# Tiles 8 to 31 of the up projection split into high and low parts by two GpSimd DMAs and a ScalarE negation

## The chip, the cores and the metric

The kernel runs on one core of a Trainium2 chip. The metric is the device time of one execution in microseconds (us). Three timed runs of the kernel before gave 833.49, 833.70 and 833.92 us; the median is 833.7 us.

## The reference

One layer of an encoder on a 512 x 1024 input, all in float32: a token-mixing sub-layer with three branches (windowed attention, spatial gating, causal pooling), a cross-attention into 256 memory tokens, and a squared-ReLU MLP, each between RMSNorms. The change touches the MLP alone:

```
hf = rmsnorm(x, g_norm[l, 4])                                # 512 x 1024
yf = jnp.square(jax.nn.relu(hf @ w_up[l])) @ w_down[l]       # w_up 1024 x 4096, w_down 4096 x 1024
x = x + rmsnorm(yf, g_norm[l, 5])
```

## The kernel before

Every matrix product is made of three TensorE products in the type float32r. An operand w is split into hi (w rounded to float32r) and lo (w minus hi), and `mm3` (L137 to 141) adds hi·hi, hi·lo and lo·hi in PSUM. The split of a weight tile is `split` (L129 to 131): a rounding copy on ScalarE writes hi, a subtraction on VectorE writes lo.

A weight tile has 128 partitions by 1024 float32 values, 512 KB. `wtile` (L112 to 119) loads it from HBM with a DMA on SyncE's queue into one of 2 buffers `wraw` and splits it into one of 8 buffers `whi` and one of 8 buffers `wlo`. The same 8 + 8 buffers also hold the operands of the second product of the MLP: the activations `ahi`, `alo` and the weights `bhi`, `blo`.

The first product of the MLP has 32 weight tiles (here U0 to U31), each 128 of the 4096 hidden features. U0 to U5 run on halves of the 512 rows and are written out by hand. From U6 on, a list `steps` orders the work: a step U makes one tile of hidden features (24 matmuls of 512 columns, then a Relu and a Square on ScalarE, L735 and L736). A step M is one of seven products of a Strassen-like scheme for the second product, for one of three groups of 8 hidden tiles (24 matmuls of 512 columns as well; its operands are sums made on VectorE and three tiles that are split, two of which are weights). In the middle of a group U and M alternate; at two places two U or two M follow each other, and U28 to U31 follow each other near the end. Then come C (sums on VectorE) and D0 and D1, the last quarter of the second product, done plainly, with eight further weight tiles through `wtile`. Four steps X at the beginning of the list transpose the residual x.

The loop over `steps` traces `prepare` for step n + 2 ahead of the matmuls of step n, so a step's tiles have their place in the buffers two steps ahead. TensorE's instructions are pinned to the order in which they are traced (`keep`, L97). The order on the other engines is made by a scheduler at compile time: it takes the work in order of priority as its inputs become ready by its own estimate of durations. Each engine, and each engine's DMA queue, runs its list in that order and waits in place.

Up to the last steps, GpSimd has small work only (a power for the norms, some sums of squares), and every DMA is issued on SyncE's queue.

Of the kernel before, what the change touches and what calls it, by code (L numbers as in the profile page):

```python
# [10 lines left out]
F32 = mybir.dt.float32  # L11
F32R = mybir.dt.float32r
AF = mybir.ActivationFunctionType
ALU = mybir.AluOpType
AX = mybir.AxisListType

P = 128
# [31 lines left out]
T_UP = T_OM + 4  # L49
# [12 lines left out]
def trunk(ctx: ExitStack, tc: tile.TileContext, xT, memT, wst, cst, vec, rows, wsp, wpl, out):  # L62
    nc = tc.nc

    per = ctx.enter_context(tc.tile_pool(name="per", bufs=1))
    wp = ctx.enter_context(tc.tile_pool(name="wp", bufs=1))
# [11 lines left out]
    def slot(name, dt=F32, shape=None):  # L78
        return sl.tile(shape or [P, S], dt, name=name, tag="slot", bufs=NSLOT)
# [7 lines left out]
    def pair(name, shape=None):  # L87
        return slot(name + "h", F32R, shape), slot(name + "l", F32R, shape)
# [16 lines left out]

    wdma = {}

    def wtiles(i):
        return [wp.tile([P, 1024], dt, name=f"w{c}{i}", tag=f"w{c}", bufs=n)
                for c, dt, n in (("raw", F32, 2), ("hi", F32R, 8), ("lo", F32R, 8))]  # L110

    def wtile(i, fence=()):  # L112
        raw, hi, lo = wtiles(i)
        wdma[i] = nc.sync.dma_start(raw, wst[i]).ins
        with ExitStack() as c:
            for ins in fence:
                c.enter_context(tc.issue_after(ins))
            split(hi, lo, raw)
        return hi, lo

    def after(i, dst, src):
# [7 lines left out]
    def split(hi, lo, src, order=free):  # L129
        return (order(nc.scalar.copy(hi, src)).ins,  # L130
                order(nc.vector.tensor_tensor(lo, src, hi.bitcast(F32), op=ALU.subtract)).ins)  # L131
# [62 lines left out]
    with ExitStack() as c1:  # L194
# [17 lines left out]
        for o in order:  # L212
            if o[0] == "x":
                nc.sync.dma_start(x0[o[1]], xT[o[1] * P:(o[1] + 1) * P, :])
            else:
                c = slice(o[2] * 512, (o[2] + 1) * 512)
# [4 lines left out]
        for o in order:  # L221
            if o[0] == "x":
                split_scaled(*xg[o[1]], x0[o[1]], vc[:, V_G + o[1]:V_G + o[1] + 1], keep)
            else:
                c = slice(o[2] * 512, (o[2] + 1) * 512)
# [8 lines left out]
        def block(i, w=None, fence=()):  # L234
            ps = bank()
            gemm(w or wtile(i, fence), xg, 0, KD, ps)
            return ps
# [103 lines left out]
        def vgate(t):  # L341
            if not wsv:
                wsv.extend(wtile(T_SV + i, fence(8 + NU0 + i)) for i in range(4))
            ps = bank()
            for k in range(KD):
                mm3(ps, cut(xg[k], t * P, (t + 1) * P), blk(wsv[k // 2], k % 2, 512), k == 0, k == KD - 1)
            vn.append(ps)
# [65 lines left out]
        def branch(n, y, sg):  # L413
            for d in range(KD):
                if d % 2 == 0:
                    w = wtile(T_BR + n * 4 + d // 2)
                ps = bank()
                gemm(w, y, 4 * (d % 2), 4, ps)
                if n == 0:
                    acc[d] = slot(f"acc{d}")  # L420
                    nc.vector.tensor_tensor(acc[d], sg[d], ps, op=ALU.mult)
                else:
                    nc.vector.tensor_tensor(sg[d], sg[d], ps, op=ALU.mult)
                    nc.vector.tensor_tensor(acc[d], acc[d], sg[d], op=ALU.add)
                if n == 2:
                    mg.append(pair(f"mg{d}"))
                    split(*mg[d], acc[d])
# [297 lines left out]
    with ExitStack() as c3:  # L725
        f = c3.enter_context(tc.tile_pool(name="f", bufs=1))
# [46 lines left out]
        def whole(name):  # L773
            return f.tile([P, 1024], F32, name=name, tag="q", bufs=8)
# [26 lines left out]
        def loads(g, *quarters):  # L801
            for ab in quarters:
                for pp in range(2):
                    i = T_DN + 8 * g + 4 * ab[0] + 2 * ab[1] + pp
                    qs[g, ab, pp] = whole(f"q{ab[0]}{ab[1]}")
                    wdma[i] = nc.sync.dma_start(qs[g, ab, pp], wst[i]).ins

        def halves(g, a):
            return rel[g, a][:, :, :HALF], rel[g, a][:, :, HALF:]
# [6 lines left out]
        def ready(g, i):  # L816

            def q(ab, pp):
                return qs[g, ab, pp]

            def new(name):
                sums[g, name] = f.tile([P, NPAIR, HALF], F32, name=name, tag="s", bufs=2)
                return sums[g, name]

            a0, a1 = halves(g, 0)
            if i == 1:
                first, second = a0, (0, 0)
            if i == 7:
                first, second = new("s3"), (0, 1)
                sub(first, a0, a1)  # L830
                for pp in range(2):
                    sub(q((0, 0), pp), q((0, 1), pp), q((0, 0), pp))
                    sub(q((0, 1), pp), q((1, 1), pp), q((0, 1), pp))
            if i > 1 and i != 7:
                b0, b1 = halves(g, 1)
            if i == 5:
                first, second = new("s1"), (0, 0)
                add(first, a1, b1)
            if i == 6:
                first, second = new("s2"), (0, 0)  # L840
                sub(first, sums[g, "s1"], a0)
                for pp in range(2):
                    sub(q((0, 0), pp), q((1, 1), pp), q((0, 0), pp))
            if i == 4:
                first, second = b1, (0, 0)
                for pp in range(2):
                    sub(q((0, 0), pp), q((0, 0), pp), q((1, 0), pp))
            if i == 3:
                first, second = sums[g, "s2"], (1, 1)
                sub(first, b0, first)  # L850
            if i == 2:
                first, second = b0, (1, 0)
            act, ws = parts(first, i), []
            for pp in range(2):
                w = tuple(wp.tile([P, 1024], F32R, name=f"b{z}{i}", tag=f"w{z}", bufs=8) for z in ("hi", "lo"))
                split(*w, q(second, pp))
                ws.append(w)
            return act, ws
# [71 lines left out]

        def prepare(st):
            if st[0] == "U":
                return wtile(T_UP + st[1])
            if st[0] == "D":
                a = st[1]
                if a == 0:
                    gy.extend(slot(f"gy{c}") for c in range(2))
                    for c in range(2):
                        nc.sync.dma_start(gy[c], rows[0:1, 1032 + c * 512:1032 + (c + 1) * 512].broadcast_to([P, 512]))
                if a == 0:  # L940
                    act = [tuple(f.tile([P, NPAIR, HALF], F32R, name=f"e{c}", tag="q", bufs=8) for c in "hl")
                           for _ in range(2)]
                    for z, src in zip(act, halves(3, a)):
                        split(*z, src)
                else:
                    act = [pair(f"e{j}") for j in range(4)]
                    for j in range(4):
                        split(*act[j], rel[3, a][:, j, :])
                ws = [wtile(T_DN + 24 + 4 * a + j) for j in range(4)]
                if a == 0:  # L950
                    for t in range(NT):
                        xt[t] = whole(f"xt{t}")
                        nc.sync.dma_start(xt[t], xd[t * P:(t + 1) * P, :])
                return act, ws
            if st[0] == "M":
                g, i = st[1:]
                if st[1:] == (0, 1):
                    loads(0, (0, 0), (0, 1), (1, 1), (1, 0))
                got = ready(g, i)
                if i == 4 and g < 2:  # L960
                    loads(g + 1, (0, 0), (0, 1))
                if i == 2 and g < 2:
                    loads(g + 1, (1, 1), (1, 0))
                return got

        got = {}
        for n in range(-2, len(steps)):
            if n >= 0 and steps[n] == ("D", 0):
                got[n + 1] = prepare(steps[n + 1])
            if n + 2 < len(steps) and n + 2 != len(steps) - 1:  # L970
                got[n + 2] = prepare(steps[n + 2])
            if n < 0:
                continue
            st = steps[n]
            if st[0] == "X":
                xturned(st[1])
            elif st[0] == "U":
                up(st[1], got.pop(n))
            elif st[0] == "M":
                product(st[1], st[2], *got.pop(n))  # L980
            elif st[0] == "C":
                combine()
            else:
                down(st[1], *got.pop(n))
# [79 lines left out]
```

## Time and profile before

| | |
|---|---|
| median of 3 runs | 833.7 us (833.49 to 833.92) |
| the profiled execution | 833.36 us |
| its span, first to last instruction | 831.6 us |
| mean granted TensorE clock over the span | 0.998 of full speed |
| busy share of the span: TensorE, VectorE, ScalarE, GpSimd | 98%, 66%, 48%, 5% |
| DMA | 88.65 MB, 107 GB/s on average |

Times in the rows are microseconds from the span's start, unless marked ns. PE is TensorE's matmul, PEld its weight load, DVE VectorE, ACT ScalarE, POOL GpSimd, SPq SyncE's queue of DMA issues. "L130" is line 130 of the kernel before. In a row of a timeline the brackets hold the time for which the engine sat idle ahead of the instruction, and what ended that wait.

### The profile page before, as it was taken

The page shows a single profiled execution, that of the slowest core. Times are in us where ns is not written, and L with a number is a line of the kernel's source. Part 1 is how long each engine was busy: PE and PEld are TensorE (multiplying, and loading weights), DVE is VectorE, ACT ScalarE, POOL GpSimd, SP SyncE. Part 2 cuts the span into 40 slices and gives each one's busy share as a digit, 9 for nine tenths or more (in the row PEclk, how much of TensorE's full clock was granted, in tenths as well). Part 3 has the DMA queues.
Part 4 walks back from the last instruction along what each step waited for, and adds up shares of the span by engine and source line. Part 5 has one row for each costly group of instructions (what it writes and reads, how often), then busy time and mean ns, then how long its engine had stood idle before and what let it go on. Part 6 is the DMA issues. An engine that isn't in the chain of part 4 may idle for free.

```text
span 831.6 us, 11071 instructions
## 1 busy us (share of the span) xinstructions
PE 817.6 (98%) x4322; PEld 700.3 (84%) x4322; DVE 544.9 (66%) x795; ACT 399.5 (48%) x696; POOL 45.2 (5%) x55
## 2 busy tenths in 40 slices
PE   8999999999999999999999999999999999999996
PEld 6888888888788888899999999788888888888885
DVE  6559893667536535718897793694719682997436
ACT  7344568432422333536466765676626452644502
POOL 0000000000000010103300041000000000000000
PEclk9999999999999999999999999999999999999999
DMA  7332112533222333402342220653421430116302
GB/s 245 127 102 76 51 54 98 186 119 102 76 102 81 121 127 102 178 1 77 102 149 102 81 78 26 254 184 136 159 77 52 158 120 26 51 44 234 103 0 102
DMA packets 27845, 88.65 MB, mean 107 GB/s; under 512 B 3344, under 2 KB 4368, under 8 KB 27792
## 3 DMA queue, kind: packets, MB, share of 16 engines
q1 hardware_dynamic: 27792, 87.94, 31.0%
q8 instruction: 34, 0.56, 0.3%
q14 instruction: 19, 0.16, 0.1%
HBM read 83.73 MB, written 4.19 MB: 106 GB/s over the span
## 4 chain that ended last, share of the span: by engine, by line
PE 88%; DVE 6%; ACT 2%; DMA 1%; issue 1%; POOL 0%; SPq 0%; POOLq 0%; DVEq 0%; ACTq 0%
PE ps L100 87%; PE ps L103 2%; DVE x L552 1%; DVE yg L551 1%; DVE wlo L131 1%; DVE m L917 1%; DVE m L799 1%; DMA q<-wst 1%; DMA x<-xT 1%; ACT sq L903 1%; ACT sq L162 0%; DVE sa L163 0%; DVE xm6l L135 0%; POOL rst L914 0%; POOL rs L176 0%
## 5 line engine op out<-in xcount | busy, mean ns | idle before, releaser
L130 ACT CAST whi<-wraw 128x1024 fp32r<-128x1024 f32 (+1 forms) x120 | 124.0, 1035 | 171.7 <-PE ps L100 113.0
L131 DVE TENSOR_TENSOR wlo<-wraw,whi 128x1024 fp32r<-128x1024 f32 (+1 forms) x120 | 145.2, 1213 | 46.5 <-ACT whi L130 46.0
L100 PE MATMUL ps<-blo,ahi 128*128 128x512 f32 x168 | 65.5, 390 | 0.8 <-DVE blo L131 0.8
L100 PE MATMUL ps<-bhi,ahi 128*128 128x512 f32 x168 | 65.6, 390 | 0.0
L100 PE MATMUL ps<-bhi,alo 128*128 128x512 f32 x168 | 65.4, 389 | 0.0
L131 DVE TENSOR_TENSOR blo<-q,bhi 128x1024 fp32r<-128x1024 f32 x42 | 50.0, 1220 | 23.5 <-ACT bhi L130 23.5
L130 ACT CAST bhi<-q 128x1024 fp32r<-128x1024 f32 x42 | 43.5, 1051 | 36.5 <-PE ps L100 17.8
L241 DVE TENSOR_TENSOR sg<-ps,rb 128x512 f32<-128x512 f32 x16 | 11.1, 692 | 49.1 <-PE ps L100 49.1
L799 DVE TENSOR_TENSOR m<-m,ps 128x512 f32<-128x512 f32 (+1 forms) x45 | 30.0, 671 | 18.8 <-PE ps L100 18.8
L100 PEld LDWEIGHTS ps<-blo,ahi 128*128 128x128 f32 x168 | 31.5, 188 | 7.6 <-DVE blo L131 1.1
L100 PEld LDWEIGHTS ps<-bhi,ahi 128*128 128x128 f32 x168 | 31.5, 188 | 6.7 <-ACT bhi L130 0.3
L100 PEld LDWEIGHTS ps<-bhi,alo 128*128 128x128 f32 x168 | 31.5, 188 | 6.6
L735 ACT ACTIVATE r<-ps 128x512 f32<-128x512 f32 (+1 forms) x38 | 19.7, 527 | 28.2 <-PE ps L100 28.1
L796 DVE TENSOR_TENSOR q<-q,q 128x1024 f32<-128x1024 f32 x24 | 28.5, 1219 | 0.0
L163 POOL TENSOR_TENSOR sb<-sb,sq 128x256 f32<-128x256 f32 x28 | 24.7, 882 | 40.9 <-ACT sq L162 40.1
L295 ACT ACTIVATE s<-s,ng 128x256 f32<-128x256 f32 x32 | 15.9, 498 | 19.2 <-DVE ng L291 19.2
L163 DVE TENSOR_TENSOR sa<-sa,sq 128x256 f32<-128x256 f32 x28 | 12.3, 439 | 16.5 <-ACT sq L162 16.2
L903 ACT ACTIVATE sq<-m,rqs 128x512 f32<-128x512 f32 (+1 forms) x9 | 6.1, 677 | 35.0 <-DVE m L799 34.7
L736 ACT ACTIVATE r<-r 128x512 f32<-128x512 f32 (+1 forms) x38 | 21.2, 568 | 0.9
L914 POOL TENSOR_TENSOR rst<-m,mhalf 128x1 f32<-128x1 f32 x4 | 2.2, 545 | 318.4 <-DVE m L799 318.4
L799 DVE TENSOR_TENSOR s<-r,r 128x1024 f32<-128x1024 f32 x3 | 3.7, 1225 | 22.9 <-ACT r L736 22.9
L163 POOL TENSOR_TENSOR ssm<-ssm,sq 128x256 f32<-128x256 f32 x7 | 8.4, 1195 | 187.9 <-ACT sq L162 187.8
(734 smaller groups left out, 2508.3 us busy)
## 6 DMA issues: line engine op xcount, KB each, us to landing
wraw<-wst SPq DMA_DIRECT2D x116, 512.0 KB, 3.2
q<-wst SPq DMA_DIRECT2D x24, 512.0 KB, 4.2
x<-xT SPq DMA_DIRECT2D x16, 256.0 KB, 5.3
xd<-xs SPq DMA_DIRECT2D x4, 512.0 KB, 3.0
xt<-xd SPq DMA_DIRECT2D x4, 512.0 KB, 5.6
out<-m SPq DMA_DIRECT2D x8, 256.0 KB, 2.1
wraw<-wst SPq DMA_DIRECT2D x4, 256.0 KB, 5.0
mt<-memT SPq DMA_DIRECT2D x8, 128.0 KB, 3.2
```

What stands on the lines that cost most here:

```text
L100: keep(nc.tensor.matmul(*args, **kw))
L103: keep(nc.tensor.transpose(o, i, ident))
L130: return (order(nc.scalar.copy(hi, src)).ins, order(nc.vector.tensor_tensor(lo, src, hi.bitcast(F32), op=ALU.subtract)).ins)
L131: order(nc.vector.tensor_tensor(lo, src, hi.bitcast(F32), op=ALU.subtract)).ins)
L163: order((eng or nc.vector).tensor_tensor(sacc, sacc, sq, op=ALU.add))
L241: nc.vector.tensor_tensor(t, ps, rb0, op=ALU.mult)
L295: nc.scalar.activation(s, s, AF.Exp, bias=ng[:, b:b + 1], scale=0.125, accum_out=den[:, b:b + 1])
L735: nc.scalar.activation(z, ps[:, :hi - lo], AF.Relu)
L736: nc.scalar.activation(z, z, AF.Square)
L796: nc.vector.tensor_tensor(o, p, q, op=ALU.subtract)
L799: nc.vector.tensor_tensor(o, p, q, op=ALU.add)
L903: nc.scalar.activation(slot("sq")[:, :n], yv, AF.Square, scale=rq32[hf][:, tb:tb + 1], accum_out=s2)
```

## The change

For U8 to U31 the tile is split without the `wraw` buffer and without VectorE. A DMA issued by GpSimd loads the tile from HBM and casts it to float32r into hi; ScalarE writes lo = -hi; a second DMA issued by GpSimd reads the same tile from HBM again and adds it to lo. The products are the same.

```diff
-    def wtiles(i):
-        return [wp.tile([P, 1024], dt, name=f"w{c}{i}", tag=f"w{c}", bufs=n)
+    def wtiles(i, whole=True):
+        return [wp.tile([P, 1024], dt, name=f"w{c}{i}", tag=f"w{c}", bufs=n) if whole or n > 2 else None
                 for c, dt, n in (("raw", F32, 2), ("hi", F32R, 8), ("lo", F32R, 8))]
...
+    def wtile_dma(i):
+
+        _, hi, lo = wtiles(i, False)
+        nc.gpsimd.dma_start(hi, wst[i])
+        nc.scalar.activation(lo, hi.bitcast(F32), AF.Identity, scale=-1.0)
+        nc.gpsimd.dma_start(lo, wst[i], accum_op=ALU.add)
+        return hi, lo
...
         def prepare(st):
             if st[0] == "U":
-                return wtile(T_UP + st[1])
+                return (wtile if st[1] < 8 else wtile_dma)(T_UP + st[1])
```

## Rows read from the trace of the kernel before

**Rows 1.** The page's first two parts: busy time, share of the span and instructions of each engine; the granted TensorE clock in 40 equal slices of the span, in tenths (9 is 90% or more).

```profile
PE 817.6 (98%) x4322; PEld 700.3 (84%) x4322; DVE 544.9 (66%) x795; ACT 399.5 (48%) x696; POOL 45.2 (5%) x55
...
PEclk9999999999999999999999999999999999999999
```

**Rows 2.** The windows view: five stretches; in each its length, then busy time (and instructions) of each engine, the granted clock, the DMA share and rate. Steps U8 to U31 lie between 546 and 780.

```profile
0.00:546.00 546.00, 539.84 (x3086) 470.01 (x3087) 356.13 (x585) 268.55 (x529) 42.97 (x51) 1.00 0.33 111
546.00:628.00 82.00, 82.00 (x363) 67.89 (x363) 48.60 (x43) 44.52 (x57) 0.00 (x0) 1.00 0.35 119
628.00:710.00 82.00, 82.00 (x364) 67.89 (x363) 56.34 (x57) 39.02 (x46) 0.00 (x0) 1.00 0.27 90
710.00:780.00 70.00, 70.00 (x311) 57.96 (x310) 57.50 (x64) 37.70 (x45) 0.00 (x0) 1.00 0.36 126
780.00:831.00 51.00, 43.80 (x205) 36.58 (x203) 26.30 (x51) 9.71 (x22) 2.18 (x4) 0.97 0.12 44
```

**Rows 3.** The waits view for TensorE, whole span, all of its rows: who waited for whom, us in total, times, longest. The row of `blo` lies at 529 us, and no row lies behind it.

```profile
PE ps L100 <- DVE wlo L131: 1.5, 1, 1.5
PE ps L100 <- DVE warm L199: 1.5, 1, 1.5
PE ps L100 <- DVE blo L131: 0.8, 1, 0.8
PE ps L100 <- DVE qt L593: 0.4, 1, 0.4
PE ps L100 <- ACT whi L130: 0.4, 1, 0.4
PE ps L100 <- POOL rs L176: 0.4, 1, 0.4
PE ps L100 <- ACT xf7h L134: 0.3, 1, 0.3
PE ps L100 <- DVE xg1l L135: 0.3, 1, 0.3
PE ps L100 <- POOL sb L163: 0.2, 1, 0.2
```

**Rows 4.** The timeline of ScalarE: three rounding copies of U tiles (U13, U21 and U29) that waited for TensorE.

```profile
584.10 1.05 ACT L130 CAST whi<-wraw 128x1024 fp32r<-128x1024 f32 x1 [2.96 <-PE ps L100]
...
665.70 1.05 ACT L130 CAST whi<-wraw 128x1024 fp32r<-128x1024 f32 x1 [3.44 <-PE ps L100]
...
747.30 1.05 ACT L130 CAST whi<-wraw 128x1024 fp32r<-128x1024 f32 x1 [3.43 <-PE ps L100]
```

**Rows 5.** The timeline of TensorE: the first matmuls of U13, U21 and U29, and of U29 also the first that reads lo.

```profile
600.45 0.39 PE L100 MATMUL ps<-xf0h,whi 128*128 128x512 f32 x1
...
682.05 0.39 PE L100 MATMUL ps<-xf0h,whi 128*128 128x512 f32 x1
...
763.65 0.39 PE L100 MATMUL ps<-xf0h,whi 128*128 128x512 f32 x1
763.88 0.39 PE L100 MATMUL ps<-xf0l,whi 128*128 128x512 f32 x1
764.10 0.39 PE L100 MATMUL ps<-xf0h,wlo 128*128 128x512 f32 x1
```

**Rows 6.** The timeline of VectorE: the subtraction that completes U29's split.

```profile
748.39 1.23 DVE L131 TENSOR_TENSOR wlo<-wraw,whi 128x1024 fp32r<-128x1024 f32 x1
```

**Rows 7.** From the view of one tile, `wraw`, between 546 and 757 us: the two halves of the split and the load's issue (duration in ns, min/median/max), and the time of these loads from issue to landing.

```profile
L130 ACT CAST whi<-wraw x23: 1040/1055/1060, 545.8 to 753.3; 128x1024 fp32r<-128x1024 f32 x23
L131 DVE TENSOR_TENSOR wlo<-wraw,whi x23: 1218/1220/1226, 547.0 to 756.7; 128x1024 fp32r<-128x1024 f32 x23
L114 SPq DMA_DIRECT2D wraw<-wst x22: 327/328/333, 548.2 to 755.6; - x22
...
DMA to landing us min/median/max: 3.1/3.2/4.8
```

**Rows 8.** The same line for the tile `q` (the weights of the M steps), 540 to 780 us.

```profile
DMA to landing us min/median/max: 3.1/4.0/5.0
```

**Rows 9.** The DMA view, 546 to 780 us: packets and bytes in all; the queue, its packets, MB and share of the 16 DMA engines; and the slowest 512 KB transfers of this stretch (median us to landing).

```profile
DMA packets 7252, 26.02 MB, mean 111 GB/s; under 512 B 800, under 2 KB 800, under 8 KB 7240
...
q1 hardware_dynamic: 7240, 25.86, 32.4%
...
xt<-xd SPq DMA_DIRECT2D x4, 512.0 KB, 5.6
```

**Rows 10.** The groups view of ScalarE, 546 to 780 us, shapes kept apart: an ACTIVATE and a CAST of 512 columns (busy us, mean ns).

```profile
L736 ACT ACTIVATE r<-r 128x512 f32<-128x512 f32 x23 | 14.6, 633 | 0.6
...
L130 ACT CAST e1h<-r 128x512 fp32r<-128x512 f32 x1 | 0.6, 622 | 0.0
```

**Rows 11.** The timeline of ScalarE where it works longest without a pause between two M steps and U17's tile is prepared.

```profile
624.96 1.05 ACT L130 CAST ahi<-s 128x1024 fp32r<-128x1024 f32 x1 [1.29 <-DVE s L799]
625.92 1.99 ACT L130 CAST bhi<-q 128x1024 fp32r<-128x1024 f32 x2
627.82 1.04 ACT L130 CAST whi<-wraw 128x1024 fp32r<-128x1024 f32 x1
628.76 1.05 ACT L130 CAST ahi<-s 128x1024 fp32r<-128x1024 f32 x1
```

**Rows 12.** The timeline of VectorE in the same stretch: the last subtraction for the M step that follows U16, and the first and the last row of a run of 18 rows without a pause.

```profile
623.70 1.23 DVE L799 TENSOR_TENSOR s<-r,r 128x1024 f32<-128x1024 f32 x1 [10.62 <-ACT r L736]
...
627.24 2.35 DVE L131 TENSOR_TENSOR blo<-q,bhi 128x1024 fp32r<-128x1024 f32 x2
...
647.80 0.68 DVE L799 TENSOR_TENSOR m<-m,ps 128x512 f32<-128x512 f32 x1
```

**Rows 13.** The timeline of TensorE: the first matmul of that M step, and the first one of U17.

```profile
633.09 0.39 PE L100 MATMUL ps<-bhi,ahi 128*128 128x512 f32 x1
...
638.53 0.39 PE L100 MATMUL ps<-xf0h,whi 128*128 128x512 f32 x1
```

**Rows 14.** The timeline of GpSimd: the last instruction ahead of the U steps and the next one.

```profile
505.39 0.71 POOL L176 TENSOR_TENSOR rs<-ms,mhalf 128x2 f32<-128x2 f32 x1 [0.94 <-DVE ms L175]
809.18 0.55 POOL L914 TENSOR_TENSOR rst<-m,mhalf 128x1 f32<-128x1 f32 x1 [303.08 <-DVE m L799]
```

**Rows 15.** The waits view of SyncE's queue, 546 to 780 us: the issues of `wraw` loads that waited for a free buffer, and for an earlier load.

```profile
SPq L114 <- DVE wlo L131: 157.2, 29, 19.0
...
SPq L114 <- DMA wraw<-wst: 4.6, 4, 2.0
```

## The prediction, made before the changed kernel had run

> **What bounds the kernel now.** First the page's busy shares: TensorE is busy 98% of the span, at the full clock in every slice [rows 1]. Then the windows view, to see where the other 2% lie. From 546 to 780 us, the stretch of U8 to U31, TensorE is busy 82.00 of 82.00, 82.00 of 82.00 and 70.00 of 70.00 us; VectorE, ScalarE and the DMA engines all have room there (at most 57.50 of 70 us, 44.52 of 82 us and a share of 0.36), and GpSimd does nothing [rows 2]. Then the waits view for TensorE: 5.4 us of waits in the whole run, the last of them 0.8 us at an M step ahead of U8, none behind it [rows 3]. So in the changed stretch the matmuls set the end, alone. Work taken from VectorE or ScalarE there buys nothing; the change can only leave TensorE's row unbroken, or break it.
>
> What it would have to be late by is read from three U tiles whose rounding copy itself waited for TensorE, that is for one of the 8 `whi` buffers to come free: U13 at 584.10, U21 at 665.70, U29 at 747.30 [rows 4]. Their first matmuls start at 600.45, 682.05 and 763.65 [rows 5]. The **lead** from a free buffer to its use is 16.35 us each time, and lo is wanted 0.45 us later, at U29's third matmul (764.10), so 16.8 us for lo. The old chain uses little of it: U29's lo is complete at 748.39 + 1.23 = 749.62, 2.3 us after the release [rows 6]; the load stands ahead of the release in `wraw`.
>
> **The change part by part.**
>
> *Removed.* 24 copies (1.05 us) and 24 subtractions (1.22 us) [rows 7]: 24 x 1.22 = 29 us of VectorE's 162 us in the stretch (48.60 + 56.34 + 57.50, [rows 2]), and on ScalarE 24 x 1.05 = 25 us, which come back as negations. The negation is an ACTIVATE of the same size; at 512 columns an ACTIVATE takes 633 ns and a CAST 622 ns [rows 10], so I take 1.05 us and ScalarE is as busy as before. Also removed: 24 issues of 0.33 us on SyncE's queue [rows 7] and the U tiles' waits for `wraw` [rows 15]. All of it is worth 0 us to the end, because TensorE waits for none of these in the stretch [rows 2, 3]. What covers them is TensorE's own row; were that gone, VectorE's 29 us would count only in part, as it is itself busy for 69% of the stretch.
>
> *Added to the DMA engines.* Each tile is read from HBM twice: 24 x 0.52 = 12.6 MB on top of 26.0 MB in the stretch. The share of the 16 engines goes from 32.4% to about 48% [rows 9]. There is room: 0 us.
>
> *Added to GpSimd's queue.* 48 issues. Nothing of GpSimd's own work lies between 506 and 809 us [rows 14], so nobody but the U tiles waits for it. Within the queue the accumulating DMA waits for ScalarE, and the next tile's casting DMA can be queued behind that wait. In the alternating part two U tiles are two steps, 10.9 us, apart, so this bites only where the first half of a chain lasts longer than that.
>
> *Added: a longer chain from the free buffer to a complete lo.* It now holds (a) the casting DMA, which can't start before `whi` is free, (n) the negation with its place in ScalarE's queue, (c) the accumulating DMA. The trace has no DMA of GpSimd's and none that casts or accumulates, so each is bounded by the 512 KB transfers it has.
> (a) Below: 3.1 us, the quickest plain load [rows 7]. Above: 5.6 us, the slowest kind in the stretch [rows 9]. I take 4.0 us, the median of the `q` loads, which run beside others as these will [rows 8].
> (n) The work is 1.05 us. The wait for ScalarE is 0 at best; at worst a whole run of other work, 624.96 to 629.81, 4.9 us [rows 11]. I take 2.0 us, so 3.05 us in all (1.05 to 5.95).
> (c) Below: a plain load again, 3.1 us. Above: it has to read two tiles and write one, so two of the slowest transfers, 11.2 us. I take two ordinary loads, 2 x 3.2 = 6.4 us [rows 7].
> Sum: 4.0 + 3.05 + 6.4 = 13.45 us against 16.8 us, so lo stands 3.35 us early and TensorE doesn't notice. The ends are 7.3 us (9.5 us early) and 22.75 us (5.95 us late).
> The Trainium skill (page "DMA: Bandwidth & Descriptors", section "Latency and other measured facts") speaks against the change: a DMA issued by GpSimd takes about 1 us to its first byte, one issued by SyncE about 0.6 us. By that page alone the chain would be an estimated 0.8 us longer, 14.25 us, still inside the lead; no run here shows it yet.
>
> *Added: a wait in ScalarE's queue.* The negation waits in place for the casting DMA, and behind it are queued the Relu and Square of finished U steps and the copies for the M steps. The tightest of those is the M step behind U16: its last lo is ready at 627.24 + 2.35 = 629.59, its first matmul starts at 633.09 [rows 12, 13], 3.5 us of cover. U17's negation falls into that very run of ScalarE (its copy stood at 627.82 [rows 11]) and its casting DMA starts only when its buffer is free, about 16.4 us ahead of 638.53 [rows 13], at 622.1. It lands at 626.1 by my value and at 627.7 by the bound. Even if it stood right ahead of the copies of 625.92, it would hold them by 1.8 us at most, inside the 3.5. So 0 us, and it is the place to look at.
>
> **Sum.** Nothing on the path: the profiled execution's 833.36 us stays. Its span of 831.6 us is 1.8 us shorter, for what lies around it, and the median of the runs is 0.34 us above it. So 833.5 us against a median of 833.7. A change of under 0.2%, 1.7 us, is about what a measurement of this kernel can't tell from none.
>
> **The rivals.**
>
> *1. The chain is longer than the lead: slower.* It decides from a + n + c = 16.8 us on. For it: casting and accumulating are unpriced in this trace, and the upper ends together give 22.75 us. Against it: my values leave 3.35 us. Its price: in the alternating part U(i)'s buffer is that of U(i-2), and between the two lies U(i-1), whose own stall lengthens the lead; so a chain that is late by e costs e/2 at each tile. Some 20 of the 24 tiles have a lead of about 16.4 us (U8, U15, U23 and U31 have more). With (c) at its upper end and the rest at my values, 18.25 us, e is 1.45 us: 20 x 0.73 = 14.5 us, 848 us. With all upper ends, e = 5.95: 20 x 2.98 = 60 us, 893 us.
>
> *2. GpSimd can't issue while VectorE works: slower.* If the issue had to wait for a pause of VectorE, the runs decide: VectorE works without a pause from 623.70 to 648.48 [rows 12], and buffers come free inside such runs. A DMA issued there would be up to 20 us late. With three such runs (one in each group) and two or three tiles in each, 8 tiles that lose some 5 us each beyond their 3.35 us cost 40 us: 873 us. For it: VectorE is busy 59 to 82% of the stretch [rows 2]. Against it: all of its long rows are subtractions and sums of two float32 operands, each only 1.2 us, and an issue could pass between two of them. The Trainium skill (page "SBUF — State Buffer", section "SBUF: two separate sides") tells of this trap: a VectorE operation that holds both ports which it shares with GpSimd keeps GpSimd from writing its DMA descriptors. Its section "Who interferes with whom" leaves a subtraction of two tensors out of it, and marks the reason as inferred; nothing in this trace can test it.
>
> *3. Faster.* Only by what TensorE waits for near the change: 0.8 us at the M step ahead of U8 [rows 3], if VectorE and SyncE's queue, relieved of U8, reach that step's operands sooner. That is 832.7 us at best, under 0.2%. For more, TensorE would have to run its matmuls faster.
>
> *4. It doesn't do what it says.* If the casting DMA copies without rounding, hi is all of w and lo is zero. The instructions, transfers and waits stay the same, and so does the time, 833.5 us.
>
> **How the numbers follow.** My forecast 0.55 and rival 4 0.05: within 0.2%, 0.60. Rival 1 0.31 and rival 2 0.06: slower by over 0.2%, 0.37. Rival 3 beyond 0.2%: 0.03. The predicted time is the forecast's, 833.5 us. The forecast's own range is 832.6 to 835.2 us. Eight in ten needs more than its 0.6: from 832.6 us up to 860 us, which takes in rival 1 to a chain of 19.4 us (e = 2.65, 20 x 1.33 = 26.5 us) and leaves out its upper end and rival 2, together about 0.15.
>
> **What the changed profile would show.** The casting DMAs should land 3 to 5.6 us after their issue, the accumulating ones about 6.4 us; U tiles' lo should be complete some 3 us ahead of the third matmul; the windows from 546 to 780 us should stay full of TensorE; VectorE's busy time should fall by 29 us, ScalarE's stay, and the HBM bytes read rise by 12.6 MB. Wrong would be: TensorE waiting for GpSimd's queue or a DMA at the first or third matmul of U steps (rival 1), issues on GpSimd's queue that end with VectorE's pauses (rival 2), or an M step waiting for its copies behind a negation.

## The result, and the profile of the changed kernel

The change made the kernel slightly slower. The median of 20 runs is 835.24 us (834.39 to 837.58), beside 833.6 us (832.92 to 835.06) of 20 runs of the kernel before. The ratio is 1.002, 95% interval 1.0013 to 1.0026, that is +1.1 to +2.2 us. The forecast was 833.5 us and no change.

The profiled execution took 834.94 us, its span 832.7 us. The first part of its page answers to [rows 1]: VectorE's time fell by 27.2 us and GpSimd's rose by 34.6, while TensorE and ScalarE kept theirs.

```profile
PE 817.5 (98%) x4322; PEld 700.3 (84%) x4322; DVE 517.7 (62%) x771; ACT 399.2 (48%) x696; POOL 79.8 (10%) x103
...
q0 software_dynamic: 6912, 25.17, 13.2%
...
HBM read 96.32 MB, written 4.19 MB: 121 GB/s over the span
```

The windows view answers to [rows 2] (length, then busy time and instructions of TensorE, its weight loads, VectorE, ScalarE, GpSimd; granted clock, DMA share, GB/s).

```profile
546.00:628.00 82.00, 82.00 (x363) 67.86 (x362) 40.06 (x36) 44.50 (x58) 11.38 (x16) 1.00 0.69 187
628.00:710.00 82.00, 82.00 (x364) 67.91 (x363) 47.66 (x49) 39.06 (x46) 11.36 (x16) 1.00 0.56 141
710.00:780.00 70.00, 70.00 (x311) 57.98 (x310) 49.15 (x55) 35.54 (x43) 9.37 (x13) 1.00 0.62 166
```

TensorE is still full there, at the full clock. In this execution its waits hold no row for a GpSimd DMA either. The most that it has on top of [rows 3] is 1.0 us for VectorE's `wlo`, at 413 us, ahead of the change, where single loads come a little earlier or later in every kernel of this study, the one before included. The next view is that of the tile `wlo` (U8 to U31): the DMAs' times to landing, and who waited.

```profile
L125 ACT ACTIVATE wlo<-whi x24: 1055/1062/1073, 540.3 to 765.8; 128x1024 fp32r<-128x1024 f32 x24
L126 POOL DMA_DIRECT2D wlo<-wst x24: 848/857/886, 541.7 to 767.2; - x24
...
DMA to landing us min/median/max: 5.0/5.2/10.0
```

The casting DMAs (tile `whi`, 540 to 775 us) landed after 3.5 to 8.0 us, median 5.2. From the issue of the casting DMA to lo complete, the median chain takes 12.6 us. 16 of the 24 are no longer than the 13.45 us forecast, and each lo lands ahead of its third matmul; so this one execution does not show the loss as a wait. Two things point to it. First, the time outside the span rose: 1.78 us before (mean of the executions, 1.72 to 1.85), 2.23 us after (2.18 to 2.28). Second, the start of the stretch is tight. GpSimd's timeline there (start, duration, and in brackets the idle time before and what ended it):

```profile
527.70 0.76 POOL L124 DMA_DIRECT2D whi<-wst  x1 [20.82 <-PE ps L100]
541.68 0.89 POOL L126 DMA_DIRECT2D wlo<-wst  x1 [13.23 <-ACT wlo L125]
542.25 0.89 POOL L124 DMA_DIRECT2D whi<-wst  x1
551.50 0.86 POOL L126 DMA_DIRECT2D wlo<-wst  x1 [8.36 <-ACT wlo L125]
552.59 0.56 POOL L124 DMA_DIRECT2D whi<-wst  x1 [0.23 <-PE ps L100]
```

U8's accumulating DMA follows its casting one by 14 us, and U9's casting DMA comes right behind it. ScalarE's timeline says why. U8's casting DMA had landed at 535.8; its negation runs 4.5 us later, behind the copies of the transposes (`xs`):

```profile
538.14 2.27 ACT L790 COPY xs<-ps 128x512 f32<-128x512 f32 x4 [1.22 <-DVE blo L139]
540.29 1.07 ACT L125 ACTIVATE wlo<-whi 128x1024 fp32r<-128x1024 f32 x1
```

In the kernel before, U8's rounding copy stood ahead of those copies:

```profile
535.93 1.05 ACT L130 CAST whi<-wraw 128x1024 fp32r<-128x1024 f32 x1
537.25 2.26 ACT L782 COPY xs<-ps 128x512 f32<-128x512 f32 x4 [0.26 <-DVE blo L131]
```

U8's lo lands at 546.90, 0.46 us ahead of its third matmul; U9's at 558.07, 0.17 us ahead. The median tile has 4.3 us. In this execution both came just in time. Its span is 1.1 us longer than that of the kernel before for other reasons: 1.0 us at 413 us and 0.2 us at its end. The experiments had to show whether they do in others, and what else costs.

### The profile page after: what moved, and what is told of

It is laid out like the page before. It is cut to its first block, busy times and chain, and to the rows that moved or that the text cites. A ratio compares the mean times of both kernels' runs of the same rounds, so it can differ in the third digit from the quotient of the medians.

```text
span 832.7 us, 11097 instructions
## 1 busy us (share of the span) xinstructions
PE 817.5 (98%) x4322; PEld 700.3 (84%) x4322; DVE 517.7 (62%) x771; ACT 399.2 (48%) x696; POOL 79.8 (10%) x103
## 4 chain that ended last, share of the span: by engine, by line
PE 86%; DVE 6%; DMA 3%; ACT 3%; issue 1%; POOL 0%; SPq 0%; POOLq 0%; DVEq 0%; ACTq 0%
PE ps L100 84%; DMA wraw<-wst 2%; PE ps L103 2%; DVE x L560 1%; DVE wlo L139 1%; DVE m L925 1%; DVE m L807 1%; DMA q<-wst 1%; DVE yg L559 1%; ACT whi L138 1%; ACT sq L911 1%; ACT sq L170 0%; DVE sa L171 0%; ACT yg L542 0%; DVE xm6l L143 0%
## 5 line engine op out<-in xcount | busy, mean ns | idle before, releaser
L138 ACT CAST whi<-wraw 128x1024 fp32r<-128x1024 f32 (+1 forms) x96 | 98.8, 1031 | 143.2 <-PE ps L100 91.3
L139 DVE TENSOR_TENSOR wlo<-wraw,whi 128x1024 fp32r<-128x1024 f32 (+1 forms) x96 | 116.2, 1213 | 42.2 <-ACT whi L138 41.4
L125 ACT ACTIVATE wlo<-whi 128x1024 fp32r<-128x1024 f32 x24 | 25.5, 1062 | 63.9 <-DMA whi<-wst 63.9
L126 POOL DMA_DIRECT2D wlo<-wst x24 | 20.6, 859 | 134.1 <-ACT wlo L125 133.2
L124 POOL DMA_DIRECT2D whi<-wst x24 | 15.6, 664 | 92.7 <-PE ps L100 92.7
```

Of the source, the lines that this page charges most:

```text
L124: nc.gpsimd.dma_start(hi, wst[i])
L125: nc.scalar.activation(lo, hi.bitcast(F32), AF.Identity, scale=-1.0)
L126: nc.gpsimd.dma_start(lo, wst[i], accum_op=ALU.add)
L138: return (order(nc.scalar.copy(hi, src)).ins, order(nc.vector.tensor_tensor(lo, src, hi.bitcast(F32), op=ALU.subtract)).ins)
```

## The experiments

Four theories were held against each other. **A**: a fixed price, paid once there are such DMAs. **B** (later **P**): a price for each of the 48 DMAs wherever it stands. **T**: a few tight tiles, whose chains end at the moment TensorE wants them. The fourth was a plain effect of measuring. Each ratio is to the kernel before, run beside it on the same chip, with its 95% interval.

**e1: the kernel before, unchanged.**

> The kernel before, unchanged, as a measure of what the comparison itself scatters. Every theory: the ratio's interval holds 1.000, the median is within 0.5 us of the other runs of the kernel before, the span some 1.8 us shorter than the time. The load that landed late near 394 us in the changed kernel's trace (5.75 us, against 4.51 before) is a matter of the run: in this second trace it may land anywhere from 4.5 to 5.8 us, and all matmuls behind 412 us shift with it by up to 0.8 us.

Measured: 833.54 us, ratio 0.9997 (0.9988 to 1.0006). The loss is not one of measuring. The time outside the span is 1.77 us.

**e2: eight plain DMAs on GpSimd's queue, off the path.** The loads of `xt` and of `gy`, from SyncE to GpSimd, `gy` in four parts:

```
-  nc.sync.dma_start(xt[t], xd[...])
+  nc.gpsimd.dma_start(xt[t], xd[...])
```

> The kernel before, with eight plain DMAs issued by GpSimd in place of SyncE late in the run, where nobody waits for them (the four loads xt and the loads gy, cut into four). Theory A (a fixed price of issuing any DMA from GpSimd: 0.45 us outside the span and about 0.3 us for eight more semaphores awaited in turn at the end): +0.7 to +0.8 us, span +0.3 us, time minus span 2.2 us in place of 1.8. Theory B (all of the loss comes from the 24 split tiles, their traffic or stalls): no change, 0.0 +- 0.3 us, time minus span 1.8 us.

Measured: 835.17 us, ratio 1.0014 (1.0006 to 1.0023), with 1.78 us outside the span. So DMAs on GpSimd's queue can cost without any chain: in the profile the last matmul to the end of the span takes 8.69 us in place of 8.07. The rest of the loss lies, in the profile, in the first 100 us (1.3 us, with a granted clock of 0.50 from 9 to 11 us, where the kernel before had 1.00), and can be chance.

**e3: tiles 10 to 27 alone (36 DMAs). e4: tiles 8, 9 and 28 to 31 alone (12 DMAs).** The six of e4 are those with the least to spare in the changed profile, near the two ends.

```
e3: (wtile if st[1] < 10 or st[1] > 27 else wtile_dma)(T_UP + st[1])
e4: (wtile_dma if st[1] in (8, 9, 28, 29, 30, 31) else wtile)(T_UP + st[1])
```

> The changed kernel with the DMA split for U10 to U27 alone (18 of 24 tiles), without U8, U9 and U28 to U31, among which are the three tiles whose lo landed within 0.5 us of its use. Theory A with stalls at the tight tiles in other runs than the profiled one: the fixed 0.75 us stays and the rest (0.9 us) goes: +0.7 to +0.8 us. Theory A alone without such stalls, the rest being scatter: also +0.75 us, but then e4 shows +0.75 as well. Theory B (in proportion to the tiles): 18/24 of 1.64 = +1.2 us.

> The changed kernel with the DMA split for U8, U9 and U28 to U31 alone (6 of 24 tiles). Theory A with stalls at the tight tiles: about the whole of the change, +1.4 to +1.8 us, and TensorE may wait at U8, U9 or U30 for a landing. Theory A without such stalls: +0.7 to +0.8 us. Theory B (in proportion to the tiles): 6/24 of 1.64 = +0.4 us.

Measured: e3 833.82 us, ratio 0.9998 (0.9988 to 1.0008); e4 836.32 us, ratio 1.0028 (1.0017 to 1.004). Eighteen tiles cost nothing that can be measured and six cost 2.4 us. A and B fall together: e3 has three quarters of the DMAs and none of the loss. In e4's profile TensorE waits for a DMA of the change (waits view). That profile is of e4's quickest execution (834.37 us), so it does not show where the rest of the 2.4 us, more than the whole change costs, was lost:

```profile
PE ps L100 <- DMA wlo<-wst: 0.3, 1, 0.3
```

**e5: tiles 8 and 9 alone. e6: tiles 28 to 31 alone. e7: the change again.**

```
e5: (wtile_dma if st[1] in (8, 9) else wtile)(T_UP + st[1])
e6: (wtile_dma if st[1] > 27 else wtile)(T_UP + st[1])
```

> The changed kernel with the DMA split for U8 and U9 alone. Theory T (the loss is TensorE waiting for the late lo of a few tiles with no room left, at the start and at the end of the stretch): U8 and U9 had 0.46 and 0.17 us to spare in the changed kernel's profile and U9's third matmul waited 0.3 us in e4's; +0.5 to +1.5 us, with a wait of TensorE for wlo at U9 (near 557 us) or U8 (near 546 us). Rival E (only the last four tiles lose, beside the eight loads for D): 0.0 +- 0.4 us.

> The changed kernel with the DMA split for U28 to U31 alone. Theory T: U30 had 0.39 us to spare in the changed kernel's profile, where its accumulating DMA took 10.0 us; +0.5 to +1.5 us, with a wait of TensorE at U30 (near 770 us). Rival S (only the first two lose): 0.0 +- 0.4 us. The sum of e5 and e6 should come near e4's +2.4 us by theory T.

> The changed kernel as it is, beside the others on the same chip. Theory T: +1.2 to +2.0 us, as measured before (1.64 us), time minus span 1.78 us as in all kernels of the last comparison, so that the 2.23 us in the first runs of the changed kernel belongs to where it ran. Theory A (a fixed price of GpSimd's DMAs outside the span): 2.23 us again.

Measured: e5 834.7 us, ratio 1.0016 (1.0000 to 1.0031); e6 834.34 us, ratio 0.9994 (0.9984 to 1.0005); e7 836.5 us, ratio 1.0026 (1.0012 to 1.004). The last four tiles cost nothing that can be measured, though U30 had but 0.39 us to spare in the changed profile; that leaves the first two, though e5's own interval only just lies above 1. By the medians alone e5 is 0.3 us above the kernel before (834.4 us on this chip). In e5 TensorE's timeline has it at U9's third matmul:

```profile
557.45 0.39 PE L100 MATMUL ps<-xf0l,whi 128*128 128x512 f32 x1
558.61 0.50 PE L100 MATMUL ps<-xf0h,wlo 128*128 128x512 f32 x1 [0.77 <-DMA wlo<-wst]
```

The twelve runs of e5 fall into two groups: seven from 833.15 to 834.79 us, five from 837.38 to 838.46 with a mean granted clock of 0.993 to 0.996, in place of 0.997. The second group is 4 us slower, far more than one wait of 0.8 us. A fall of the clock can do that. One shows in e6's profiled run (838.29 us), behind a gap of 1.72 us at 394 us, a place that the change doesn't touch (columns as above; first e6, then the kernel before):

```profile
392.00:395.00 3.00, 1.74 (x13) 1.33 (x11) 3.00 (x4) 1.15 (x4) 1.06 (x1) 1.00 0.25 52
395.00:400.00 5.00, 4.51 (x25) 4.51 (x26) 3.60 (x7) 2.47 (x6) 1.44 (x2) 0.67 0.59 189
400.00:420.00 20.00, 19.97 (x154) 19.71 (x153) 15.27 (x30) 9.14 (x19) 8.19 (x8) 0.91 0.23 78
...
392.00:395.00 3.00, 1.47 (x12) 1.27 (x12) 3.00 (x5) 2.04 (x7) 1.04 (x2) 1.00 0.56 175
395.00:400.00 5.00, 4.94 (x42) 4.74 (x42) 2.64 (x7) 2.07 (x3) 1.40 (x2) 1.00 0.66 212
```

After a stretch with TensorE busy 1.74 of 3 us, 25 matmuls run where the kernel before runs 42, at a mean granted clock of 0.67; it stands at 0.50, the lower of its two levels (1.2 GHz, not 2.4), from 397 to 403 us. The gap alone does not decide it: the kernel before is busy 1.47 of 3 us at the same place (a gap of 1.53 us), e1 has a gap of 1.72 us, and neither falls. The profiles of e9 and e11 do fall there (0.50 from 395 to 397 and from 396 to 398 us, behind gaps of 1.73 us). So e5's second group can have lost its time there as well; no profile caught a fall behind U9's wait, and what set that group back stays open.

**e8: the accumulating DMA issued twice for each tile.** Lo then holds 2w - hi in place of w - hi; the work of the engines is the same.

```
     nc.gpsimd.dma_start(lo, wst[i], accum_op=ALU.add)
+    nc.gpsimd.dma_start(lo, wst[i], accum_op=ALU.add)
```

> The changed kernel with the accumulating DMA issued twice for each tile, one after the other (lo then holds 2w - hi, which changes the result; the matmuls are the same). It makes the chain longer by one accumulating DMA, some 5.2 us and its issue, 12.6 to about 18.4 us in the middle tiles, past the 16.8 us of the lead: e = 1.6 us. Theory T with the e/2 rule of the prediction: 20 x 0.8 = 16 us, and some 5 us more at each of the three tight tiles, so +15 to +40 us, TensorE waiting for wlo at the third matmul of most U steps. Rival (the lead is longer than I read it, as GpSimd's queue can run further ahead): under +5 us.

Measured: 891.48 us. TensorE's waits, and the windows of the stretch:

```profile
PE ps L100 <- DMA wlo<-wst: 40.0, 15, 5.4
```

```profile
546.00:628.00 82.00, 70.70 (x292) 56.85 (x291) 35.32 (x32) 38.32 (x50) 15.85 (x21) 0.94 0.84 201
628.00:710.00 82.00, 72.02 (x301) 57.97 (x300) 39.48 (x41) 32.35 (x37) 14.12 (x19) 0.96 0.73 167
710.00:838.00 128.00, 109.29 (x446) 87.50 (x445) 63.19 (x68) 50.97 (x62) 22.98 (x30) 0.95 0.73 167
```

With some 5 us more in a chain that has 4 to spare, TensorE waits 15 times for a lo. The size was missed: 57 us (beside 834.4 us on the same chip, and e8 has one execution alone) against at most 40. The waits are 40.0 us, and TensorE's own busy time rose from 817.6 to 835.3, 17.7 us, at a granted clock of 0.94 to 0.96 in these windows, where the kernel before has 1.00 [rows 2]. By these means, an estimate, the clock alone took 82 x 0.06 + 82 x 0.04 + 128 x 0.05 = 14.6 us of that. The expectation had no term for the clock.

**e9: tiles 10 to 31 (44 DMAs). e10: tiles 9 to 31 (46). e11: all 24, tile 8 recorded early. e12: the change again.** In e11 tile 8's load and negation are recorded ahead of the transposes X2 and of the loads of the M step in front of U8; TensorE's order is the same.

```
e9:  (wtile if st[1] < 10 else wtile_dma)(T_UP + st[1])
e10: (wtile if st[1] < 9 else wtile_dma)(T_UP + st[1])
e11:
+    if n == 4:
+        got[8] = prepare(steps[8])
-    if n + 2 < len(steps) and n + 2 != len(steps) - 1:
+    if n + 2 < len(steps) and n + 2 not in (8, len(steps) - 1):
```

> Tiles 10 to 31 are split by DMAs (44 GpSimd DMAs instead of 48); tiles 8 and 9 keep the load on SyncE and the split on ScalarE and VectorE. Theory T (late first chains: U8's negation stands behind the xs copies in ScalarE's queue, U9's casting DMA behind U8's accumulating one in GpSimd's queue, and TensorE waits at the third matmul of U8 or U9): no wait of TensorE on a wlo written by DMA, so nothing lost inside the span and at most the 0.45 us outside the span; ratio 1.000 to 1.001, 833.5 to 834.3 us beside a kernel before of 833.6. Rival P (each GpSimd DMA has its price, or some number between 36 and 48 of them has one): 44 of 48 keep nearly the whole loss, ratio about 1.002, +1.5 to 2 us. The time outside the span tells apart by itself whether the 0.45 us come with the number of DMAs (then 2.2 us already at 44) or with tiles 8 and 9 (then 1.8).

> Tiles 9 to 31 are split by DMAs; tile 8 is not. Theory T with the queue as U9's cause: the casting DMA of U9 no longer stands behind an accumulating DMA of U8, is issued when its buffer comes free (about 540.5 us instead of 542.25), and U9's lo lands over 1.5 us ahead of its third matmul; no wait, nothing lost inside the span, ratio 1.000 to 1.001. Variant T2 (U9 is late by its own transfers: its casting DMA takes 7.9 us beside the loads of M05): a wait of 0.1 to 1 us of TensorE on U9's wlo stays, ratio 1.0005 to 1.0015. Rival P: 1.002.

> All 24 tiles are split by DMAs, as in the change, but the load and negation of tile 8 are recorded four steps earlier (ahead of the transposes X2, and so ahead of the loads of M07): its negation stands ahead of the xs copies in ScalarE's queue. TensorE's order is the same. Theory T: U8's lo lands over 4 us ahead of its third matmul, U9's casting DMA is issued as soon as its buffer is free, no wait of TensorE on a wlo written by DMA; what is left is the 0.45 us outside the span and 0.2 us at the end: ratio 1.0003 to 1.001, +0.3 to 0.8 us, against +1.6 to 2.1 of the change itself in the same runs. Rival P (the price of 48 DMAs wherever they stand): as the change, 1.002 to 1.0026. If the time outside the span falls to 1.8 too, it belonged to the first two tiles.

> The change itself once more, for a comparison with the three others on the same chip. Theory T and rival P alike: ratio 1.002 to 1.0026, +1.6 to 2.1 us, time outside the span 2.2 us, and in the profiled run U8 or U9 with under 0.5 us to spare or a short wait of TensorE there.

Measured: e9 834.0 us, ratio 1.0008 (0.9995 to 1.0021); e10 834.05 us, 1.0004 (0.9995 to 1.0013); e11 834.85 us, 1.0017 (1.0008 to 1.0026); e12 835.38 us, 1.002 (1.0011 to 1.0028). Without tile 8 the loss is 0.3 us by the medians, and 0.22 us of that lie outside the span (2.00 us against 1.78). For e12 the waits view and TensorE's timeline again show U9:

```profile
PE ps L100 <- DMA wlo<-wst: 0.9, 1, 0.9
```

```profile
558.82 0.50 PE L100 MATMUL ps<-xf0h,wlo 128*128 128x512 f32 x1 [0.92 <-DMA wlo<-wst]
```

In e10, U9's casting DMA is issued as soon as TensorE frees its buffer:

```profile
540.63 0.76 POOL L124 DMA_DIRECT2D whi<-wst  x1 [33.81 <-PE ps L100]
549.45 0.89 POOL L126 DMA_DIRECT2D wlo<-wst  x1 [8.05 <-ACT wlo L125]
```

It lands after 7.4 us, the accumulating one after 7.9, and 0.68 us are left: no wait, but less than the 1.5 us expected. So both causes count for U9: GpSimd's queue, which took some 1.4 us of its lead (in the changed kernel the issue came at 542.25, with the matmuls 0.2 us later than here), and its own slow transfers beside other loads (variant T2 in part). In e11 the negation stands ahead of the `xs` copies, and U9's casting DMA has GpSimd's queue and the DMA engines without U8's second DMA:

```profile
515.96 0.76 POOL L124 DMA_DIRECT2D whi<-wst  x1 [7.96 <-PE ps L100]
534.88 0.89 POOL L126 DMA_DIRECT2D wlo<-wst  x1 [18.15 <-DVE q L804]
542.13 0.56 POOL L124 DMA_DIRECT2D whi<-wst  x1 [6.37 <-PE ps L100]
550.76 0.86 POOL L126 DMA_DIRECT2D wlo<-wst  x1 [8.07 <-ACT wlo L125]
```

U8 now has 7.2 us to spare and U9 3.6, and TensorE waits for neither. The loads of the next M step are there in e11 too, and yet U9's DMAs take 4.9 and 5.2 us. What e11 lacks is one more transfer of 512 KB beside the casting DMA: in e10 a `wraw` load issued at 540.71, in the changed kernel U8's accumulating DMA, in flight from 541.68 to 546.90. The wait is gone as T says. Yet the time is 1.15 us above the kernel before, not 0.3 to 0.8: between the two forecasts, and only 0.5 us below e12, with intervals that overlap.

**e13: 48 small DMAs without a chain. e14: e11 again. e15: the change again.** e13 is the kernel before, with this in place of the tile's preparation:

```
w = wtile(T_UP + st[1])
if st[1] > 7:
    for z in range(2):
        nc.gpsimd.dma_start(spare[z], w[z][:, :16].bitcast(F32))
return w
```

> The kernel before, with two GpSimd DMAs more for each of tiles 8 to 31, 48 in all: each copies 16 columns of the tile's hi or lo, once written, into a spare tile that nobody reads. No chain of the change is in it; its number of DMAs on GpSimd is. Reading N (what is left of the loss without the late first tiles is the price of 48 GpSimd DMAs, 0.45 us outside the span and about 0.25 us of semaphores at its end): time outside the span 2.2 us against 1.78, +0.5 to 0.9 us, ratio 1.0006 to 1.0011. Reading K (the time outside the span comes with the kind or size of the DMAs, casting and accumulating of 512 KB): outside 1.8 us, +0 to 0.4 us. If all of the change's loss were the number of DMAs: +1.6 to 2.1 us, ratio 1.002.

> All 24 tiles by DMAs with tile 8 recorded early, again, beside the change on another chip. The run before gave a ratio of 1.0017, 95% interval 1.0008 to 1.0026, between the two forecasts. Theory T with the price of 48 DMAs (0.45 us outside, 0.25 us at the end): +0.5 to 0.9 us, ratio 1.0006 to 1.0011, and less than the change by 0.7 to 1.4 us. If the early tile is worth nothing: as the change, +1.6 to 2.1 us.

> The change itself, beside the two others on the same chip: ratio 1.002 to 1.0026, +1.6 to 2.1 us, outside the span 2.2 us, U8 or U9 with under 0.5 us to spare or a wait of TensorE there.

Measured: e13 834.67 us, ratio 1.0009 (1.0 to 1.0018); e14 835.05 us, 1.0018 (1.0009 to 1.0027); e15 835.21 us, 1.0023 (1.0008 to 1.0038). The time outside the span is 1.77 us in e13, 2.23 in e14, 2.22 in e15: reading K for that term, it does not come with the number of DMAs. But in its profile e13 pays at the span's end. VectorE's last instruction ends 3.2 us ahead of the end of the span in the kernel before (826.88 + 1.54 of 831.6), 3.4 in the changed kernel (827.79 + 1.54 of 832.7) and 3.9 in e13 (span 831.8):

```profile
826.37 1.54 DVE L918 SCALAR_TENSOR_TENSOR m<-yg,rr,xt 128x512 f32<-128x512 f32 x3
```

In e15 the same wait is there once more:

```profile
558.48 0.39 PE L100 MATMUL ps<-xf0l,whi 128*128 128x512 f32 x1
559.86 0.50 PE L100 MATMUL ps<-xf0h,wlo 128*128 128x512 f32 x1 [0.99 <-DMA wlo<-wst]
```

**All profiles together.** TensorE runs the same 4322 matmuls in the same order in all these kernels (e8, whose waits run through the whole stretch, is left out below). So one can subtract the start of each matmul from the start of the same one in the kernel before, and read how much is lost from 545 to 560 us, where U8 and U9 begin:

| kernels | lost from 545 to 560 us |
|---|---|
| tiles 8 and 9 in the change's order: after, e4, e5, e7, e12, e15 | 0.03, 0.61, 1.11, 0.51, 1.21, 1.35 us |
| neither tile, or 9 alone: e1, e2, e3, e6, e9, e10, e13 | 0.00 us in each |
| tile 8 early: e11, e14 | 0.00 us in both |

From 560 us to the last matmul none of these 15 differs from the kernel before by more than 0.04 us. The other differences lie ahead of the change: in the first 100 us (-0.96 to +1.28 us), from 391 to 415 us (-0.2 to +3.2 us) and at 528 us (-0.3 to +0.4 us). They come in kernels with and without the change, and are the scatter of the runs. The largest go with the clock: e6, e9 and e11 lose 3.2, 1.7 and 1.5 us at the fall near 396 us.

## Why the prediction was wrong

**What bounds the kernel, and what the removal brings:** right. (The waits of [rows 3] add up to 5.8 us, not 5.4; nothing hangs on it.) TensorE sets the end, VectorE's time fell by 27.2 us (29 forecast), ScalarE's stayed, and none of it was worth anything. 12.6 MB more were read, and there was room, though the share of the DMA engines rose further than to 48%: to 0.56 to 0.69. The DMA view of the changed kernel from 546 to 780 us shows the dearer packets of GpSimd's queue (packets, MB, share): 45.4% for 24.18 MB, where 25.86 MB of plain loads had taken 32.4% [rows 9].

```profile
q0 software_dynamic: 6655, 24.18, 45.4%
q1 hardware_dynamic: 4039, 14.19, 16.9%
```

**The chain, 13.45 us against 16.8:** right for the median tile, in part by luck, as the errors of the terms cancel in part. (a) was too small: 5.3 us, not 4.0, and up to 8.1, beyond the bound of 5.6, as it meets other transfers. (n) was too large for most: the negation starts within 0.1 us of the landing for 20 of 24 tiles, so 1.4 us from the landing to the next issue, not 3.05. (c) was too large in the middle, 5.2 us in place of 6.4, and up to 10.0. The median chain, 12.6 us, leaves 4.3 us. The 0.4 us to the first byte by which the Trainium skill ("DMA: Bandwidth & Descriptors", "Latency and other measured facts") sets GpSimd's DMAs behind SyncE's fits the quickest casting DMA, 3.5 us, 0.4 us above the quickest plain load [rows 7]. It need not be the cast: e2's four plain loads of `xt` on GpSimd's queue, 512 KB each, took 3.6 us at best, though four are few.

**The wait in ScalarE's queue** was held to 1.8 us for the copies behind U17's negation, without the 1.05 us of the negation itself; 2.8 us would still be inside the 3.5. No M step waited. It is the negations that waited for ScalarE: U17's and U25's 2.7 us, U8's 4.5.

**The step that failed** is the one on GpSimd's queue: it "bites only where the first half of a chain lasts longer than" 10.9 us, and that was then costed at nothing, with U8 counted among the tiles that have more lead. U8's first half lasts 14 us, from 527.70 to 541.68. The two terms of (n) and the queue were each bounded (the 4.5 us in ScalarE's queue are inside the 4.9 of [rows 11]), but applied to tiles in the alternating part. At the start of the stretch the steps are others: copies of the transposes stand in ScalarE's queue, and U8's negation waits behind them. That left U8 with nearly nothing in spite of its longer lead, and handed the delay to U9 by GpSimd's order. U9 then met slow transfers, 7.9 to 8.2 us for casting and 6.6 to 7.7 for accumulating (after, e12, e15), so (a) failed with it, beyond its bound of 5.6 us; e10 shows that these alone leave U9 only 0.68 us. Where two U steps follow each other the queue bit too, without loss: the casting DMAs of U13, U21 and U29 were issued right behind an accumulating one, and these tiles had 1.5, 2.5 and 1.8 us to spare. Rival 1 named this outcome and its mark, TensorE waiting for a DMA at a third matmul; it has the right mechanism for two tiles and not for twenty.

**What was not in the sum at all:** the time around the span, +0.45 us, and its end, +0.2 us, where the sum said that what lies around the span stays.

The loss adds up so: 0.78 us of wait at U8 and U9 (mean of the four profiles of the change: 0.03, 0.51, 1.21, 1.35), 0.2 us at the end, 0.45 us outside, together 1.4 of the 1.64 us measured (1.1 to 2.2). e9 and e10 bear this out from the side of leaving tile 8 out. For e11 and e14, whose profiles have no wait, 0.65 us should remain, but they measured +1.15 and +1.49, with intervals that reach down to +0.7; the medians alone do not tell them from the change. The clock may account for the gap. Six of 11 executions of e11 and of e14 have a mean granted clock below 0.997 (9 of 35 and 6 of 27 of the kernel before beside them), and e11's own profile falls near 396 us, where it has nothing of the change. Counting the executions at 0.997 or more alone, on both sides, e11 stands 0.7 us above the kernel before (5 against 26 executions) and e14 0.7 (5 against 21), as the sum says, and the change 1.9 (e12), 1.5 (e15) and 1.5 (e7). But the groups are small, the division was made with the results at hand, and it is not clean: by the same count e13 loses nothing (4 executions), e5 0.2 (7) and e6 0.7 us (9), where the sum would want about 0.8 for e5 and nothing but its end for e6. So the waits at U8 and U9 are shown by the traces, and the times of e11 and e14 agree with them only on this reading. Why the clock falls oftener in some kernels stays open, and so does the cause of the time outside the span: 1.78 us in e1 to e6, in e13 with 48 small DMAs and in e8 with 72 of 512 KB, 2.00 with 44 and 46, and 2.22 with 48.

**Rival 2** is out. The accumulating DMA is issued 0.3 us after the negation's end for all 24 tiles, and during 17 of these issues VectorE is at work. That agrees with the exception for the subtraction of two tensors in the Trainium skill ("SBUF — State Buffer", "Who interferes with whom"). **Rival 3** is out as well: no profile of the change gains at the M step ahead of U8. **Rival 4** would not show in a time.

No version beat the kernel before. Of those that keep the change, e3 (18 tiles) costs nothing that can be measured.

## What to carry to other kernels

A budget of lead and chain that holds for the steady state says nothing of the first tiles: work out the first and the last chain from the rows of their own steps, and look at what is recorded ahead of them in each engine's queue. Where two halves of a chain share one queue in order, a late first half is handed on to the next tile, whose own lead looked ample. When an engine is full and nothing is gained by relieving the others, each of these small terms can show in the time, the end and the surroundings of the span among them. And where the effect is 1 to 2 us, look at the granted clock of each execution before you read a median: a fall elsewhere in the kernel costs as much.

## What the runs showed of the hardware

- A casting DMA of 512 KB issued by GpSimd landed after 3.5 us at best and up to 8.5 beside others (e10's U13); an accumulating one after 5.0 at best and up to 10.9 (e11's U30). Issuing one took 0.56 to 0.89 us on GpSimd, against 0.33 us on SyncE's queue [rows 7].
- A wait of TensorE can cost more than its length: in e8 the granted clock was 0.94 to 0.96 in the windows with waits, and TensorE's busy time grew by 17.7 us beside 40.0 us of waits.
- The end of the span, from the last matmul's start to the last instruction, changes with DMAs on GpSimd's queue, and neither by their bytes nor by their number: 8.07 us without any, 8.2 to 8.3 in the change and in e4, e8, e9, e10, e11 and e14 (12 to 72 of 512 KB), 8.5 with 8 of 512 KB at the last four tiles (e6), 8.7 with 8 plain loads (e2), 8.8 with 48 small ones (e13), but 7.9 and 8.0 with 36 and 4 whose last is issued at 732 and 551 us (e3, e5). One profile each; the cause is open.
- In the same place and behind gaps of much the same length the granted clock fell to 0.50 in three profiles (e6, e9, e11: 1.72, 1.73 and 1.73 us) and stayed at 1.00 in others (e1 1.72, the kernel before 1.53).
